# One inference layer on one core: the order of a few steps in the start-up, and the engine for one addition

## The chip, the core and the metric

The kernel runs on one core of a Trainium2 chip. The core has TensorE (PE in the profile), which multiplies matrices out of SBUF into PSUM, three engines that work on vectors, VectorE (DVE), ScalarE (ACT) and GpSimd (POOL), and SyncE (SP), whose queue issues most transfers. Each engine runs its own list of instructions in order; semaphores hold an instruction back until what it needs is there. The metric is the time of one execution in microseconds on the device, as the median of the runs.

## The reference

One layer of a decoder trunk, for a prompt of 1024 rows and 8 sample rows, 1024 columns wide (`D`). The parts that the change touches are the norm of x, the projection into `u, v, z_a, ...` and the product of the per-layer embedding p with `w_ple`:

```python
xn = _rmsnorm(h, pre_g)
proj = jnp.einsum('bld,de->ble', xn, w_in)
u, v, z_a, x_b, z_b, g_a, g_b = jnp.split(proj, SPLITS, axis=-1)
...
h = h + _rmsnorm(jnp.einsum('bld,de->ble', m, w_out), post_g)
e = jnp.einsum('blp,pd->bld', p, w_ple)
gate = jax.nn.sigmoid(jnp.einsum('bld,de->ble', _rmsnorm(h, ple_in_g), w_pg))
h = h + _rmsnorm(gate * e, ple_out_g)
```

Between them stand a gated mix along chunks of 128 rows, a pooling branch over trailing windows, and two projections that are merged by sigmoid gates. All is in float32.

## The kernel before, in words

**Tiling.** x comes as eight tiles of 128 rows (`x_89` to `x_92` are the last four, in the names that the built program gives) and one of the 8 sample rows (`xe_84`). Each row is scaled by the root of its mean square (`norm_root`, `norm_scale`, L853 to L859): ScalarE squares and sums, VectorE adds epsilon, GpSimd takes the root (`rstd`), VectorE scales the tile in place. The scaled tiles are turned by TensorE against an identity matrix, so that the contraction lies along the partitions. `x_half(j, kp)` (L872) does this for four tiles (`j` = 0: rows 0 to 511, 1: rows 512 to 1023) and two blocks of 128 columns (`kp` = 0 to 3, called first to fourth block here): eight transposes into PSUM. The result is called `pst`.

**Precision and products.** A float32 operand is split into two parts: a high one that ScalarE rounds (`xB11h`, `ph`, `wehi`), and the rest, the low one, that VectorE makes (`xB11l`, `pl`, `welo`). A product takes three matmuls, high by high, low by high and high by low. The large projections are done as seven products of sums of quarters instead of eight products of quarters. So the kernel needs both the parts of x's quarters and x's quarters as wholes, for the sums: the wholes lie in the buffer `big`. `x_out` (L900) writes a whole from PSUM on ScalarE (`big<-pst`), `x_whole` (L906) adds a high and a low part back together on GpSimd (`big<-xB11h,xB11l`), for x's first half of columns and rows. `xB22h` and `xB22l` are the parts of the second half of both.

**The sample's row.** `x_extra` (L911) turns the eight sample rows into one bank of PSUM (`pxe`), and VectorE multiplies them by the norm's gains into `big`, in four instructions. `x_tail` (L919) splits them into high and low parts.

**p and its product.** `p_turn(1, q)` turns p's second half, rows 512 to 1023, four transposes into one bank (`pp`); ScalarE and VectorE make `ph` and `pl` of it. `embed(t)` multiplies tile t's part by `w_ple` into a region of PSUM (`e`, 12 matmuls), and `embed_out(t)` copies it out, on ScalarE unless another engine is given. For tile 4 it is `nc.vector`.

**PSUM.** Two kinds of buffers are handed out in turn as they are asked for: three regions of two banks (`acc`, `e`, `pst` of the blocks 2 to 4), and two single banks (`pxe`, `pp`, `pst` of the first block). Who asks for a buffer waits for the last use of the one it gets.

**The weights of v.** VectorE makes sums of loaded weights (`vs<-vraw`) and low parts (`vw<-vraw,vw` or `vw<-vs,vw`), ScalarE the high parts. Products of x's parts with `vw` go to `acc`; `steps[n].evacuate()` copies them out (`v<-acc`). `steps[2]` and `steps[3]` are one product of each of the first two pairs of v's columns; in the built program the second pair's product lies in `acc_186` and its copy in `v_195`.

**What sets the order.** All operations go through a class `Planner`, whose call at L301 issues them, so that every instruction has line L301. What `begin()` (L1743) calls is fixed: each engine plays it in the order in which it was written. What comes after `plan.fixed = False` is put in order by the planner's own costs and due times. The place of the change is in the last third of `begin()`.

Of the kernel before, what the change touches and what calls it, by code (L numbers as in the profile page):

```python
# [13 lines left out]
ALU = mybir.AluOpType  # L14
# [7 lines left out]
HALF = 512  # L22
# [285 lines left out]
def hybrid_step(  # L308
# [7 lines left out]
    nc = tc.nc  # L316
# [24 lines left out]
    def bank(name):  # L341
        n_name[0] += 1
        return plan.tile(bankp.tile([P, 512], F32, tag="bank", name=f"{name}_{n_name[0]}"), "bank")

    def region(name):

        n_name[0] += 1
        return plan.tile(accp.tile([P, 2, 512], F32, tag="acc", name=f"{name}_{n_name[0]}"), "acc")
# [3 lines left out]
    def split(src, hi, lo):  # L352

        nc.scalar.activation(out=hi, in_=src, func=AF.Copy)
        nc.vector.tensor_tensor(out=lo, in0=src, in1=f32(hi), op=ALU.subtract)
# [4 lines left out]
    def add(out, a, b):  # L360
        nc.vector.tensor_tensor(out=out, in0=a, in1=b, op=ALU.add)
# [12 lines left out]
    nc = plan  # L374
# [43 lines left out]
    def quarter(kp, j):  # L418
        both = big[:, 2 * kp : 2 * kp + 2, :].rearrange("p a t -> p (a t)")
        return (both[:, 2 * HALF :] if j else both[:, : 2 * HALF]).rearrange("p (k t) -> p k t", k=2)  # L420
# [449 lines left out]
    col = lambda i, k: gvec[:, i * NB + k : i * NB + k + 1]  # L870

    def x_half(j, kp):  # L872

        if kp == 0:
            ps = [bank("pst") for _ in range(2)]
        else:
            ps = region("pst")
            ps = [ps[:, kk] for kk in range(2)]
        for kk in range(2):
            k = 2 * kp + kk  # L880
            for i in range(4):
                nc.tensor.transpose(ps[kk][:, i * P : (i + 1) * P], xts[4 * j + i][:, k * P : (k + 1) * P], ident)
        if j and kp < 2:
            turned[j, kp] = ps
            return
        hi, lo = x_parts(j, kp)
        for kk in range(2):
            nc.scalar.activation(out=hi[:, kk, :HALF], in_=ps[kk], func=AF.Copy, scale=col(0, 2 * kp + kk))
        for kk in range(2):
            nc.vector.scalar_tensor_tensor(out=lo[:, kk, :HALF], in0=ps[kk], scalar=col(0, 2 * kp + kk),  # L890
                                           in1=f32(hi[:, kk, :HALF]), op0=ALU.mult, op1=ALU.subtract)
        turned[j, kp] = ps

    turned = {}

    def x_parts(j, kp):
        what = f"B{kp // 2 + 1}{j + 1}"
        return xop.parts[what, kp % 2] if (what, kp % 2) in xop.parts else xop.new(what, kp % 2)

    def x_out(j, kp):  # L900

        for kk, ps in enumerate(turned.pop((j, kp))):
            o, gain = quarter(kp, j)[:, kk, :HALF], col(0, 2 * kp + kk)
            nc.scalar.activation(out=o, in_=ps, func=AF.Copy, scale=gain)

    def x_whole(j, kp):  # L906

        hi, lo = (f32(x[:, :, :HALF]) for x in xop.parts[f"B{kp // 2 + 1}{j + 1}", kp % 2])
        nc.gpsimd.tensor_tensor(out=quarter(kp, j)[:, :, :HALF], in0=hi, in1=lo, op=ALU.add)

    def x_extra():  # L911
        ps = bank("pxe").rearrange("p (k t) -> p k t", k=NB)
# [6 lines left out]
    def x_tail():  # L919
        for kp in range(2, NB // 2):  # L920
            split(quarter(kp, 1)[:, :, HALF:], *(x[:, :, HALF:] for x in x_parts(1, kp)))
# [410 lines left out]
    steps = [vsteps[i][j] for pairs in ((0, 1), (2, 3)) for j in range(2) for i in pairs]  # L1332
# [367 lines left out]
    def embed_terms(t, n, terms):  # L1700

        if t == 2:
            e_ps[t, n] = e_ps.get((t, n)) or bank("e")
        elif t not in e_ps:
            e_ps[t] = region("e")
        out = e_ps[t, n] if t == 2 else e_ps[t][:, n]
        todo = left.setdefault((t, n), 6)
        for k, (i, j) in terms:
            nc.tensor.matmul(out, pcut[t // 4][i][:, k, t % 4 * P : (t % 4 + 1) * P], we.at(n, k)[j],
                             start=todo == 6, stop=todo == 1)  # L1710
            todo -= 1
        left[t, n] = todo

    def embed(t):
        for n in range(2):
            embed_terms(t, n, [(0, HH), (0, HL), (0, LH), (1, HH), (1, HL), (1, LH)])

    def embed_out(t, by=None):
        e = slot("e", (P, 2, HALF))
        if t == 2:  # L1720
            for n in range(2):
                nc.scalar.activation(out=e[:, n], in_=e_ps.pop((t, n)), func=AF.Copy)
        elif by is None:
            nc.scalar.activation(out=e, in_=e_ps.pop(t), func=AF.Copy)
        else:
            by.tensor_copy(out=e, in_=e_ps.pop(t))
        r = t // 2 * 2 * P
        dma(kept["e"][r : r + 2 * P].rearrange("(p i) (n c) -> i p n c", i=2, n=2)[t % 2], e)
# [14 lines left out]
    def begin():  # L1743
        psl = slot("psamp", (P, PLE))
        p_load(0, 0)
        for i, v in enumerate((pre_g, pool_scale, ple_in_g)):
            dma(vecs[i * NB : (i + 1) * NB, :], v[0].rearrange("(k p) -> k p", p=P), nc.scalar)
        we.fetch(0)
        we.fetch(1)
        p_load(0, 1)  # L1750
        for t in range(4):
            x_load(t)
        dma(xe[:NS], x_sample)
        steps[0].loads()
        steps[1].loads()
        for t in range(4, NB):
            x_load(t)
        for q in range(2):
            p_load(1, q)
        dma(psl[:NS], p_sample)  # L1760
        praw.append(psl)
        fetched[0] = 6
        early_loads()

        def busy(n):
            ps = region("warm")[:, 0]
            for _ in range(n):
                nc.tensor.matmul(ps, junk[:, :P], junk, start=True, stop=True)

        p_new(0)  # L1770
        busy(5)
        we.high(0, 0)
        p_turn(0, 0, (0,), nc.vector)
        busy(1)
        p_turn(0, 0, (1,))
        we.high(0, 1)
        for k in range(2):
            we.low(0, k)
        for k in range(2):
            for i in (HH, LH):  # L1780
                for t in range(2):
                    embed_terms(t, 0, [(k, i)])
        for t in range(2):
            embed_terms(t, 0, [(0, HL), (1, HL)])
        for k in range(2):
            we.high(1, k)
        for k in range(2):
            we.low(1, k)
        vps = bank("vecs")
        nc.tensor.transpose(vps[:, : 3 * NB], vecs[: 3 * NB, :], ident[: 3 * NB, : 3 * NB])  # L1790
        nc.vector.tensor_copy(gvec, vps[:, : 3 * NB])
        embed_terms(0, 1, [(0, HH), (0, LH), (1, HH), (1, LH)])
        p_turn(0, 1)
        embed_terms(0, 1, [(0, HL), (1, HL)])
        embed_terms(1, 1, [(0, HH), (0, LH), (1, HH), (1, LH), (0, HL), (1, HL)])
        norm_root(0)
        norm_root(1)
        norm_scale(0)
        embed(2)
        norm_root(2)  # L1800
        embed_out(0, nc.vector)
        norm_root(3)
        norm_scale(1)
        norm_scale(2)
        embed_out(1)
        embed(3)
        norm_scale(3)
        embed_out(2)
        vweights[0].prepare("A11")
        embed_out(3, nc.vector)  # L1810
        for kp in range(3):
            x_half(0, kp)
        vweights[1].prepare("A11")
        x_half(0, 3)
        steps[0].run()
        vweights[0].prepare("A12")
        vweights[1].prepare("A12")
        norm_root(4)
        steps[0].evacuate()
        steps[1].run()  # L1820
        norm_root(S)
        norm_root(5)
        steps[1].evacuate()
        norm_scale(4)
        norm_root(6)
        norm_scale(S)
        norm_root(7)
        for t in range(5, NB):
            norm_scale(t)
        x_whole(0, 0)  # L1830
        x_whole(0, 1)
        steps[2].run()
        steps[2].evacuate()
        x_out(0, 3)
        x_out(0, 2)
        steps[3].run()
        for t in (8, 4, 5):
            steps[t].loads()
        steps[8].loads = None
        x_extra()  # L1840
        steps[3].evacuate()
        p_new(1)
        p_turn(1, 0)
        x_half(1, 2)
        p_turn(1, 1)
        x_half(1, 3)
        x_tail()
        embed(4)
        x_out(1, 2)
        x_half(1, 0)  # L1850
        x_out(1, 0)
        embed_out(4, nc.vector)
        x_out(1, 3)
        x_half(1, 1)
        x_out(1, 1)
        vweights[0].add_up()
        xop.combine("T3")
        embed(5)
        embed_out(5)
        prepared[0] = 4  # L1860
# [52 lines left out]
```

## Time and profile before

| | |
|---|---|
| three runs | 979.62, 979.65 and 981.12 us, median 979.65 |
| the profiled execution | 980.18 us |
| its span, first to last instruction | 978.4 us |
| mean clock granted to TensorE in it | 0.996 of full speed |
| instructions of PE, DVE, ACT, POOL | 6077, 1263, 899, 143 |

All times in the profile are microseconds from the start of the span. A row of a timeline gives start, duration, engine, line, operation, output and inputs, the size (partitions by elements) and the count of instructions that were put together; in square brackets stand the idle time before it and what ended that. Instructions of an engine overlap at their ends, so a duration is a little more than the distance from one start to the next. A granted clock of 0.50 is half speed.

### The profile page before, as it was taken

How to read it: one execution, taken by the hardware profiler on the slowest of the kernel's cores; microseconds unless marked ns; L12 is line 12 of the kernel's file. 1: busy time of each engine (PE TensorE's matmuls, PEld its weight loads, DVE VectorE, ACT ScalarE, POOL GpSimd, SP SyncE). 2: the span in 40 equal slices, each digit the busy share in tenths (PEclk: the TensorE clock that was granted, in tenths of full speed). 3: DMA queues.
4: the chain of work that ended last, by engine and by line, in shares of the span. 5: the costliest groups of instructions: out<-in, count | busy, mean ns of one | idle time of the engine just before them, and what ended most of it. 6: DMA issues, size and time to landing. Idle time of an engine off the chain costs nothing. (4 is left out here: it accounts for less than half of the span.)

```text
span 978.4 us, 16078 instructions
## 1 busy us (share of the span) xinstructions
PE 964.9 (99%) x6077; PEld 860.4 (88%) x6077; DVE 799.1 (82%) x1263; ACT 532.3 (54%) x899; POOL 73.2 (7%) x143
## 2 busy tenths in 40 slices
PE   9999999999999999999999999999999999999996
PEld 6789999999999999999999999999999986888775
DVE  6796658887789698979897987697799799769786
ACT  6775998865444433344543333552363273967662
POOL 1400000000000000001000100000000001312222
PEclk9999999999999999999999999999999999999999
DMA  9445572422483253656735167884583393799966
GB/s 334 160 151 129 135 171 87 167 94 78 141 298 130 95 187 118 242 196 221 258 131 173 37 228 249 273 312 151 176 302 107 126 349 97 169 280 363 292 183 194
DMA packets 119308, 185.56 MB, mean 190 GB/s; under 512 B 29183, under 2 KB 75735, under 8 KB 119222
## 3 DMA queue, kind: packets, MB, share of 16 engines
q1 hardware_dynamic: 117102, 177.11, 53.8%
q0 software_dynamic: 2080, 7.41, 4.3%
q8 instruction: 48, 0.79, 0.3%
q14 instruction: 30, 0.25, 0.1%
q10 hardware_dynamic: 48, 0.01, 0.0%
HBM read 125.85 MB, written 53.87 MB: 184 GB/s over the span
## 5 line engine op out<-in xcount | busy, mean ns | idle before, releaser
L301 DVE TENSOR_TENSOR u<-acc,u 128x520 f32<-128x520 f32 (+1 forms) x84 | 58.3, 695 | 23.8 <-PE acc L301 21.9
L301 POOL TENSOR_TENSOR rstd<-ms,mhalf 128x1 f32<-128x1 f32 (+1 forms) x36 | 29.7, 825 | 230.1 <-DVE ms L301 208.7
L301 POOL MEMSET u<- 128x8 f32 x32 | 3.3, 104 | 491.3 <-PE acc L301 232.2
L301 ACT ACTIVATE u<-acc 128x512 f32<-128x512 f32 x36 | 21.4, 594 | 23.7 <-PE acc L301 23.1
L301 ACT ACTIVATE paw<-pas 128x512 fp32r<-128x512 f32 x16 | 10.1, 628 | 30.7 <-DVE pas L301 25.5
L301 ACT ACTIVATE pbw<-pbs 128x512 fp32r<-128x512 f32 x16 | 10.0, 629 | 29.3 <-DVE pbs L301 26.1
L301 DVE TENSOR_TENSOR v<-acc,v 128x520 f32<-128x520 f32 (+1 forms) x20 | 13.9, 693 | 12.8 <-PE acc L301 12.6
L301 ACT ACT_TABLE_LOAD x17 | 21.8, 1283 | 4.3 <-PE acc L301 1.8
L301 DVE TENSOR_TENSOR big<-big 128x1024 f32<-128x1024 f32 (+4 forms) x20 | 23.7, 1217 | 0.0
L301 ACT ACTIVATE big<-v 128x1024 uint16<-128x1024 uint16 x16 | 18.6, 1170 | 7.2 <-DMA v<-vw 7.2
L301 PE MATMUL accm<-qh,wpoolw 128*128 128x260 f32 (+1 forms) x96 | 20.9, 320 | 0.0
L301 ACT ACTIVATE zbw<-zbs 128x512 fp32r<-128x512 f32 x16 | 10.0, 628 | 16.5 <-DVE zbs L301 10.2
L301 ACT ACTIVATE gbw<-gbs 128x512 fp32r<-128x512 f32 x16 | 10.0, 624 | 15.7 <-DVE gbs L301 13.7
L301 DVE TENSOR_TENSOR big<-mix,big 128x256 f32<-128x256 f32 x32 | 12.7, 419 | 6.9 <-ACT big L301 6.8
L301 ACT ACTIVATE big<-mix 128x256 f32<-128x256 f32 x32 | 11.7, 379 | 12.4 <-PE mix L301 12.0
L301 DVE TENSOR_TENSOR acc<-acc,u 128x512 f32<-128x512 f32 (+1 forms) x16 | 11.2, 699 | 8.8 <-PE acc L301 8.8
L301 ACT ACTIVATE uw<-us 128x512 fp32r<-128x512 f32 x16 | 10.0, 626 | 14.0 <-DVE us L301 6.8
L301 ACT ACTIVATE vw<-v 128x1024 uint16<-128x1024 uint16 x16 | 16.2, 1045 | 2.3 <-DVE v L301 2.3
L301 PEld LDWEIGHTS accm<-qh,wpoolw 128*128 128x128 f32 x96 | 15.6, 188 | 1.9
L301 ACT ACTIVATE u<-u 128x1032 f32<-128x1032 f32 (+1 forms) x8 | 6.8, 853 | 18.9 <-DVE u L301 18.8
L301 ACT ACTIVATE gb<-gb 128x1032 f32<-128x1032 f32 (+1 forms) x8 | 6.8, 854 | 18.5 <-DVE gb L301 18.5
L301 ACT ACTIVATE zaw<-zas 128x512 fp32r<-128x512 f32 x16 | 10.1, 629 | 12.4 <-PE acc L301 5.2
(666 smaller groups left out, 3599.7 us busy)
## 6 DMA issues: line engine op xcount, KB each, us to landing
ga<-ga SPq DMA_DIRECT2D x16, 516.0 KB
gb<-gb SPq DMA_DIRECT2D x16, 516.0 KB
vraw<-in_w_in_dram SPq DMA_DIRECT2D x22, 256.0 KB
ya<-za SPq DMA_DIRECT2D x8, 516.0 KB
yb<-zb SPq DMA_DIRECT2D x8, 516.0 KB
x<-in_x_prompt_dram SPq DMA_DIRECT2D x8, 512.0 KB
e<-e SPq DMA_DIRECT2D x8, 512.0 KB
garaw<-in_w_in_dram SPq DMA_DIRECT2D x8, 512.0 KB
```

The source lines that it names most:

```text
L301: getattr(getattr(self.nc, e), method)(*args, **kwargs)
```

## The change

- `x_half` is cut in two: `x_turn`, the transposes, and `x_cut`, the parts on ScalarE and VectorE. Elsewhere `x_half` still calls both in a row.
- `x_whole` adds on VectorE instead of GpSimd. Its first call comes after `x_extra` (before: after the scales of x's tiles), its second after `x_tail`.
- `steps[3].evacuate()` is called ahead of `x_extra` instead of behind it.
- The third block of x's second half is turned ahead of p's second half, and its fourth block between p's two groups; the parts are made where they were made before.
- The copy of tile 4's `e` goes to ScalarE, and is asked for one place earlier.

```diff
     def x_half(j, kp):
+        x_turn(j, kp)
+        x_cut(j, kp)
+
+    def x_turn(j, kp):
...
+        turned[j, kp] = ps
+
+    def x_cut(j, kp):
+
         if j and kp < 2:
-            turned[j, kp] = ps
             return
-        hi, lo = x_parts(j, kp)
+        ps, (hi, lo) = turned[j, kp], x_parts(j, kp)
...
-        turned[j, kp] = ps
...
-        nc.gpsimd.tensor_tensor(out=quarter(kp, j)[:, :, :HALF], in0=hi, in1=lo, op=ALU.add)
+        add(quarter(kp, j)[:, :, :HALF], hi, lo)
...
         for t in range(5, NB):
             norm_scale(t)
-        x_whole(0, 0)
-        x_whole(0, 1)
...
         steps[3].run()
+        steps[3].evacuate()
...
         x_extra()
-        steps[3].evacuate()
+        x_whole(0, 0)
+        x_turn(1, 2)
         p_new(1)
         p_turn(1, 0)
-        x_half(1, 2)
+        x_cut(1, 2)
+        x_turn(1, 3)
         p_turn(1, 1)
-        x_half(1, 3)
+        x_cut(1, 3)
         x_tail()
+        x_whole(0, 1)
         embed(4)
         x_out(1, 2)
         x_half(1, 0)
+        embed_out(4)
         x_out(1, 0)
-        embed_out(4, nc.vector)
```

What that does to the engines' lists is seen in the built programs. TensorE before, from the sample's transposes (`pxe_207`) on; `pp_210` and `pp_214` are p's two groups, `pst_211` x's third block:

```order
L301 MATMUL pxe_207<-ident,xe_84 128x8 x8
L301 MATMUL pp_210<-ident,p_124 128x128 x4
L301 MATMUL pst_211<-ident,x_89 128x128
L301 MATMUL pst_211<-ident,x_90 128x128
L301 MATMUL pst_211<-ident,x_91 128x128
L301 MATMUL pst_211<-ident,x_92 128x128
L301 MATMUL pst_211<-ident,x_89 128x128
```

TensorE now, from the same place; the third block is `pst_208`, p's first group `pp_211`, the fourth block `pst_214`:

```order
L301 MATMUL pxe_207<-ident,xe_84 128x8 x8
L301 MATMUL pst_208<-ident,x_89 128x128
L301 MATMUL pst_208<-ident,x_90 128x128
L301 MATMUL pst_208<-ident,x_91 128x128
L301 MATMUL pst_208<-ident,x_92 128x128
L301 MATMUL pst_208<-ident,x_89 128x128
L301 MATMUL pst_208<-ident,x_90 128x128
L301 MATMUL pst_208<-ident,x_91 128x128
L301 MATMUL pst_208<-ident,x_92 128x128
L301 MATMUL pp_211<-ident,p_124 128x128 x4
L301 MATMUL pst_214<-ident,x_89 128x128
```

The third block has moved ahead of p's first group, and the fourth ahead of its second. `pp_211` waits for the same multiplies of `pxe_207` on VectorE as `pp_210` did, since it has the same bank.

VectorE at that place, the difference of its list (`x_92` is x's last tile, `e_221` the copy of tile 4's `e`):

```order
 L301 TENSOR_SCALAR x_92<-x_92,rstd_203 128x1024
 L301 TENSOR_TENSOR big<-pxe_207,gvec 128x2x8 x4
-L301 TENSOR_TENSOR pl_209<-pp_210,ph_208 128x2x256
-L301 SCALAR_TENSOR_TENSOR xB22l_213<-pst_211,gvec,xB22h_212 128x512 x2
-L301 TENSOR_TENSOR pl_209<-pp_214,ph_208 128x2x256
-L301 SCALAR_TENSOR_TENSOR xB22l_217<-pst_215,gvec,xB22h_216 128x512 x2
+L301 TENSOR_TENSOR big<-xB11h_166,xB11l_167 128x1024
+L301 TENSOR_TENSOR pl_210<-pp_211,ph_209 128x2x256
+L301 SCALAR_TENSOR_TENSOR xB22l_213<-pst_208,gvec,xB22h_212 128x512 x2
+L301 TENSOR_TENSOR pl_210<-pp_215,ph_209 128x2x256
+L301 SCALAR_TENSOR_TENSOR xB22l_217<-pst_214,gvec,xB22h_216 128x512 x2
```

One addition is new there, behind the multiplies; the rest keeps its order under new numbers. Further down the second addition takes the place of the copy `e_221`, which stands on ScalarE now, behind its copies of the third block (`big<-pst_208`). GpSimd's two additions are gone from its list, between its last root and its first memset (of an end of `v`). ScalarE's copy `v_195<-acc_186` has not moved: it stands behind the copies `big<-pst_171` and ahead of `ph` in both programs, though it is now written ahead of the sample's row. SyncE's list is the same.

## The prediction

> **What bounds the kernel now.** I read the page first, then the waits of PE, then the timeline around PE's longest wait. The page gives the span and the busy time of each engine.
>
> ```profile
> span 978.4 us, 16078 instructions
> PE 964.9 (99%) x6077; PEld 860.4 (88%) x6077; DVE 799.1 (82%) x1263; ACT 532.3 (54%) x899; POOL 73.2 (7%) x143
> ```
>
> PE is busy for 99% of the span, so time can be won only where PE stops or runs slowly. The waits of PE over the whole run, with the total, the number and the longest of each:
>
> ```profile
> PE pp L301 <- issue: 2.3, 1, 2.3
> PE warm L301 <- DVE junk L301: 1.3, 1, 1.3
> PE e L301 <- ACT wehi L301: 1.0, 1, 1.0
> ```
>
> Only the first lies where the change is: PE stops once, for 2.3 us, ahead of p's second half (`pp`). The releaser is given as "issue", so the timeline must name it. PE's rows there:
>
> ```profile
> 33.32 0.66 PE L301 MATMUL pxe<-ident,xe 8*128 8x8 f32 x8
> 36.30 1.09 PE L301 MATMUL pp<-ident,p 128*128 128x128 f32 x4 [2.32 <-issue]
> 37.17 1.91 PE L301 MATMUL pst<-ident,x 128*128 128x128 f32 x8
> 38.88 0.85 PE L301 MATMUL pp<-ident,p 128*128 128x128 f32 x4
> 39.56 1.04 PE L301 MATMUL pst<-ident,x 128*128 128x128 f32 x8
> 40.35 0.48 PE L301 MATMUL e<-wehi,ph 128*128 128x512 f32 x1
> ```
>
> And what VectorE and GpSimd do at that time:
>
> ```profile
> 31.69 1.42 DVE L301 TENSOR_SCALAR x<-x,rstd 128x1024 f32<-128x1024 f32 x2
> 33.18 2.69 DVE L301 TENSOR_SCALAR x<-x,rstd 128x1024 f32<-128x1024 f32 x1
> 35.79 0.41 DVE L301 TENSOR_TENSOR big<-pxe,gvec 128x16 f32<-128x16 f32 x4
> 32.82 5.26 POOL L301 TENSOR_TENSOR big<-xB11h,xB11l 128x1024 f32<-128x1024 f32 x2
> ```
>
> The sample's transposes end at 33.98 (33.32 + 0.66). `pp` reuses their bank, so it waits until VectorE's four multiplies have read them, at 36.20 (35.79 + 0.41). These queue behind VectorE's last scale of x, which takes 2.69 us where two others take 1.42 together (0.71 to 0.75 each). All of it lies beside GpSimd's adds of x's halves. So the stall is GpSimd's add, passed on: add, slow scale, late multiplies, late bank.
>
> Then the clock. Columns: length, busy time and count of each engine, granted clock, DMA share, GB/s.
>
> ```profile
> 5.24:8.65 3.41, 2.38 (x10) 1.64 (x10) 2.43 (x6) 2.26 (x4) 0.00 (x0) 1.00 1.03 381
> 18.89:22.31 3.42, 3.42 (x31) 3.36 (x30) 3.31 (x6) 3.25 (x6) 0.00 (x0) 1.00 1.02 395
> 22.31:25.72 3.41, 3.41 (x15) 2.50 (x14) 3.41 (x7) 3.41 (x7) 0.00 (x0) 1.00 1.07 340
> 32.54:35.95 3.41, 1.44 (x12) 0.93 (x10) 3.34 (x4) 2.27 (x5) 3.41 (x3) 1.00 0.88 232
> 35.95:39.37 3.42, 3.08 (x15) 3.11 (x16) 0.93 (x4) 0.84 (x2) 2.71 (x18) 0.50 0.06 12
> 43.66:79.00 35.34, 35.34 (x207) 30.90 (x206) 35.16 (x47) 23.46 (x36) 0.00 (x0) 1.00 0.41 130
> ```
>
> From 35.95 to 39.37 PE gets half its clock; in the other rows it gets all of it. The stretch before, of the same 3.41 us, has PE busy for only 1.44; one with 2.38 busy (5.24 to 8.65) is not followed by half a clock. So the stall is paid twice: as idle time, and as 24 transposes at half speed.
>
> **The change, part by part.** *The stall.* The adds leave GpSimd, so the last scale should take 0.75 and end at 33.93 instead of 35.87. x's third block (8 transposes) now comes ahead of p's and needs no bank of the sample's; its fourth transpose is the first to need that scale. How long a transpose takes at full clock:
>
> ```profile
> 18.38 3.65 PE L301 MATMUL pst<-ident,x 128*128 128x128 f32 x32
> 21.79 0.48 PE L301 MATMUL acc<-xB11h,vw 128*128 128x512 f32 x1
> ```
>
> 32 of them fill 18.38 to 21.79, so 0.107 each. The fourth is due at 33.98 + 3 x 0.107 = 34.30, 0.37 after the scale. The multiplies then end at 34.45, and `pp` comes at 33.98 + 8 x 0.107 = 34.84, 0.39 after them. The stall goes whole: **2.32 us**.
>
> *The clock.* 24 transposes now take 36.30 to 40.35, 4.05 us; at full clock 24 x 0.107 = 2.56. That saves **1.49 us**. The lower bound comes from the 16 transposes in the next row, which take 1.89 with their changes of bank (0.118 each): 4.05 - 24 x 0.118 = 1.22.
>
> [...]
>
> *The sum.* 2.32 + 1.49 = 3.81, if nothing else is late: `e`'s first product then starts at 36.54 instead of 40.35.
>
> *What is next late.* Rows of PE, VectorE and ScalarE after the gap:
>
> ```profile
> 43.22 1.91 PE L301 MATMUL pst<-ident,x 128*128 128x128 f32 x16
> 45.11 0.50 PE L301 MATMUL e<-wehi,ph 128*128 128x512 f32 x1
> 42.35 1.40 DVE L301 SCALAR_TENSOR_TENSOR xB22l<-pst,gvec,xB22h 128x512 fp32r<-128x512 f32 x2
> 43.66 0.25 DVE L301 TENSOR_TENSOR xB22l<-big,xB22h 128x16 fp32r<-128x16 f32 x2
> 43.83 1.22 DVE L301 COPY e<-e 128x1024 f32<-128x1024 f32 x1
> 44.97 0.68 DVE L301 TENSOR_TENSOR vs<-vraw 128x512 f32<-128x512 f32 x1
> ```
>
> ```profile
> 37.48 0.60 ACT L301 ACTIVATE ph<-pp 128x512 fp32r<-128x512 f32 x1 [2.67 <-PE pp L301]
> 40.28 0.60 ACT L301 ACTIVATE ph<-pp 128x512 fp32r<-128x512 f32 x1
> 40.76 1.28 ACT L301 ACTIVATE xB22h<-pst,gvec 128x512 fp32r<-128x512 f32 x2
> 41.90 0.34 ACT L301 ACTIVATE xB22h<-big 128x16 fp32r<-128x16 f32 x2
> 42.11 1.29 ACT L301 ACTIVATE big<-pst,gvec 128x512 f32<-128x512 f32 x2
> 48.26 1.03 ACT L301 ACTIVATE e<-e 128x1024 f32<-128x1024 f32 x1 [0.82 <-PE e L301]
> ```
>
> ScalarE: `ph` followed `pp`'s end (37.39) by 0.09, so now it starts at 34.84 + 4 x 0.107 + 0.09 = 35.36. From start to start, by these rows, `ph` costs 0.48, a pair of highs 1.14, the two small ones 0.21, the two copies of a block 1.14. The string ph, highs, ph, highs, small ones, block copies is 0.48 + 1.14 + 0.48 + 1.14 + 0.21 + 1.14 = 4.59, so the copy of `e`, which the change moves here from VectorE, starts at 39.95 and ends at 40.98. PE needs that bank 45.11 - 40.35 = 4.76 after `e`'s start, at 41.30: 0.32 to spare. The last 8 transposes of the row at 43.22 need the block's region half a row earlier, at 36.54 + 2.87 + 0.95 = 40.36; its copies end at about 40.1, some 0.25 to spare. So this edit costs nothing, but a delay of 0.3 us on ScalarE would show.
>
> VectorE: the first add (taken at 1.22, by the row at 43.83, VectorE's work on the same 1024 columns) runs 34.4 to 35.65, ahead of `pl`, which cannot start before `ph` ends at 35.96: hidden. After it `pl` (0.68, like the 128x512 of the row at 44.97), lows 1.40, `pl`, lows, small ones 0.25 follow without a gap, each some 0.08 under the one before, to about 40.6. The second add takes the very place and 1.2 us of the copy of `e` that left. `vs` then starts at about 41.7 instead of 44.97: 3.25 earlier, not 3.81. The next rows show two weights of VectorE's and PE's first use of each:
>
> ```profile
> 66.24 0.68 DVE L301 TENSOR_TENSOR vw<-vraw,vw 128x512 fp32r<-128x512 f32 x1
> 70.96 0.62 PE L301 MATMUL acc<-xT4h,vw 128*128 128x512 f32 x2
> 75.22 0.69 DVE L301 TENSOR_TENSOR vw<-vs,vw 128x512 fp32r<-128x512 f32 x1
> 76.61 0.63 PE L301 MATMUL acc<-xT2h,vw 128*128 128x260 f32 x4
> ```
>
> That matters, since VectorE works 35.16 of the 35.34 us from 43.66 to 79.00, and PE uses what it makes. The closest use I found: `vw` ends at 75.91 (75.22 + 0.69) and PE reads it at 76.61, 0.70 later. The shortage of 3.81 - 3.25 = 0.56 leaves 0.14 of it. So VectorE just keeps up. Further on, the order differs only in two weights that VectorE makes one step later and one evacuation that ScalarE does one step earlier. I take these at nothing: one step is 0.7 to 1.2, and the first of those weights ends at 66.92, 4.0 ahead of its use at 70.96. PE stops nowhere, so the rest shifts as a whole.
>
> *The copy of the second pair,* written ahead of the sample's row, stands at the same place on ScalarE in both built orders, and the sample's row and p's first group share one bank as before. It costs nothing and gains nothing.
>
> *GpSimd's memsets* came after its adds and now come right after its last root, beside the scale that was slow:
>
> ```profile
> 38.06 0.56 POOL L301 MEMSET rc<- 128x1 f32 x15
> ```
>
> At worst they hold the scale for all of their 0.56 us, which is 0.2 more than its 0.37 to spare; at best not at all, as tiny writes. I take nothing, and keep 0.2 for the range. SP's transfers keep their order.
>
> **The rivals.** *The clock is not won.* Either the median run, unlike the profiled one, never lost it, since the 3.41-us stretches can fall otherwise in another run: then 3.81 - 1.49 = 2.32 are won. Or transposes don't count as work for the clock: then the stretch from 32.54 still holds only the 0.8 us of products up to 33.32, the next one stays at half, and at half clock 3.41 us lose 1.7: 2.1 are won. Off the two starting times that is 977.3 to 978.1. Against the second: 18.89 to 22.31 is nearly all transposes, and the stretch after it has clock 1.00. [...] Together 0.14.
>
> *VectorE or ScalarE is late in part.* A margin of 0.14 to 0.39 breaks for one or two of the four places above, and 0.2 to 2 of the gain go back as new stops: 977.5 to 979.5. 0.07.
>
> *The change doesn't do what it says.* The scale stays slow for another reason than the add. Then the fourth transpose waits until 35.87, a gap of 1.57, and 21 transposes at half clock follow to about 39.7: 0.65 won, 979.2. For it: the row names no cause. Against it: its two neighbours, without the add, took half of 1.42. 0.04.
>
> *Slower: VectorE becomes the bound.* Its string from `vs` to the `vw` at 75.22 doesn't start earlier (a late load of v's weights would do it). Then PE stops there, for 3.81 - 0.70 = 3.1 us, and, as at 33.98, a clock of one half follows, for 1.5 (as above) to 1.7 (half of 3.41): 3.8 - 3.1 - 1.6 = -0.9, 980.9. It decides from where the string is less than about 1 us earlier. Against it: the DMA share is down to 0.06 from 35.95 to 39.37, so those loads should be in. 0.03.
>
> **How the numbers follow.** The profiled execution took 980.18 us and the median of the runs is 979.65, 0.53 less. 980.18 - 3.81 = 976.4, and 979.65 - 3.81 = 975.8; I give 976.1, with 0.72. Own range: 975.3 (the median's figure and another 0.53) to 976.9 (the profiled figure with 0.27 less for the clock and 0.2 for the memsets). To leave out no more than 2 in 10 it must take in the clock rival: 975.3 to 978.1. 0.2%, about what a measurement of this kernel can tell from no change, is 1.96 us, so faster means below 977.69: the forecast, half of the clock rival and a little of the third, 0.82. Same: the other half, most of the partial cases and the 0.04: 0.14. Slower: 0.04.
>
> **What would show it.** Right: the scale ahead of the sample's multiplies takes 0.75; PE has no wait at `pp`; the granted clock is 1.00 from 32 to 43; `e` starts 3.8 earlier against the sample's transposes. The steps are wrong one by one if the scale still takes over 2 us; if the clock falls with no gap; or if the waits of PE show a new entry, at `e` or `pst` for ScalarE or at `acc` for `vw`. A time above 978.1 would make the prediction wrong.

## The result, and the profile after

The changed kernel takes 975.82 us (median of six runs, 975.26 to 976.12) where the kernel before takes 979.63: 3.81 us less, a ratio of 0.9958 with the 95% interval 0.9945 to 0.9971. In two later sets of runs, each beside the kernel before, it was 2.77 and 3.81 us faster. The profiled execution took 976.12 us, with a span of 974.4.

The waits of TensorE in it. The stop of 2.3 us at `pp` is gone, and no other of its kind has come into the list:

```profile
PE warm L301 <- DVE junk L301: 1.3, 1, 1.3
PE pp L301 <- DMA p<-in_p_prompt_dram: 0.2, 1, 0.2
```

(The `pp` of 0.2 is p's first half, in the first 10 us. The wait for `wehi` in the kernel before, 1.0 there, lies in the first 10 us too; it hangs on a load (ScalarE stands idle 0.99 for it), and over the traces it was anything from too short for the list to 1.2.)

TensorE at the place of the change:

```profile
33.19 0.66 PE L301 MATMUL pxe<-ident,xe 8*128 8x8 f32 x8
33.78 1.09 PE L301 MATMUL pst<-ident,x 128*128 128x128 f32 x8
34.71 0.60 PE L301 MATMUL pp<-ident,p 128*128 128x128 f32 x4
35.15 1.04 PE L301 MATMUL pst<-ident,x 128*128 128x128 f32 x8
36.02 0.60 PE L301 MATMUL pp<-ident,p 128*128 128x128 f32 x4
36.38 0.48 PE L301 MATMUL e<-wehi,ph 128*128 128x512 f32 x1
...
39.25 2.06 PE L301 MATMUL pst<-ident,x 128*128 128x128 f32 x16
41.13 0.50 PE L301 MATMUL e<-wehi,ph 128*128 128x512 f32 x1
```

The sample's transposes end at 33.85 (33.19 + 0.66) and `e` starts at 36.38. These two times make the measure that I use for every kernel below: **2.53 us** now, 6.37 before (33.98 to 40.35). The other 13.2 us up to the first `acc` that follows, and the 925 us behind that, are as they were.

The clock, over the time in which it had fallen before (length, busy time and count of each engine, granted clock, DMA share, GB/s):

```profile
33.00:36.00 3.00, 3.00 (x30) 2.79 (x29) 2.41 (x6) 2.26 (x6) 0.46 (x18) 1.00 0.90 239
36.00:39.40 3.40, 3.40 (x20) 2.78 (x19) 2.90 (x5) 3.40 (x9) 0.00 (x0) 1.00 0.10 25
39.40:42.80 3.40, 3.40 (x24) 2.91 (x22) 3.37 (x7) 3.40 (x7) 0.00 (x0) 1.00 0.25 104
```

VectorE, with the scale that had taken 2.69 as the last of the first row's three, and GpSimd:

```profile
31.55 2.45 DVE L301 TENSOR_SCALAR x<-x,rstd 128x1024 f32<-128x1024 f32 x3
33.92 0.40 DVE L301 TENSOR_TENSOR big<-pxe,gvec 128x16 f32<-128x16 f32 x4
34.25 1.21 DVE L301 TENSOR_TENSOR big<-xB11h,xB11l 128x1024 f32<-128x1024 f32 x1
36.04 0.69 DVE L301 TENSOR_TENSOR pl<-pp,ph 128x512 fp32r<-128x512 f32 x1 [0.58 <-ACT ph L301]
...
41.74 0.68 DVE L301 TENSOR_TENSOR vs<-vraw 128x512 f32<-128x512 f32 x1
```

```profile
32.66 0.35 POOL L301 MEMSET v<- 128x8 f32 x1
32.70 0.72 POOL L301 MEMSET rc<- 128x1 f32 x15
```

Three scales from 31.55 to 34.00; the multiplies follow at once, and the addition stands in the gap ahead of `pl`.

### The profile page after: what moved, and what is told of

It reads as the page before. It is cut to its first block, busy times and chain, and to the rows that moved or that the text cites. A ratio compares the mean times of both kernels' runs of the same rounds, so it can differ in the third digit from the quotient of the medians.

```text
span 974.4 us, 16073 instructions
## 1 busy us (share of the span) xinstructions
PE 964.2 (99%) x6077; PEld 859.2 (88%) x6077; DVE 798.1 (82%) x1264; ACT 533.9 (55%) x900; POOL 67.9 (7%) x141
```

## The experiments

**The theory:** GpSimd's first addition holds VectorE's last scale, this the multiplies, these the bank that p's first group needs; TensorE stops for 2.3 us and then pays again with half a clock. **The rivals:** the order on TensorE (p ahead of the block) is what cost the time, wherever the addition runs; the half clock has another cause than the stop, or no part in the gain. The table gives the time from the sample's transposes to `e` in each trace, and the medians with those of the kernel before in the same set.

| kernel | to `e` | median | before | ratio, 95% |
|---|---|---|---|---|
| before, again | 6.43 | 980.24 | 980.68 | 0.9989 to 1.0008 |
| changed | 2.53 | 975.82 | 979.63 | 0.9945 to 0.9971 |
| changed, second | 2.53 | 976.96 | 979.73 | 0.9953 to 0.9978 |
| changed, third | 2.53 | 976.87 | 980.68 | 0.9951 to 0.9979 |
| p first | 3.16 | 977.47 | 979.74 | 0.9963 to 0.9980 |
| p first, again | 3.15 | 976.49 | 979.73 | 0.9954 to 0.9979 |
| additions on GpSimd | 5.88 | 978.28 | 979.74 | 0.9976 to 0.9992 |
| copy on VectorE | 2.53 | 977.93 | 979.74 | 0.9965 to 0.9987 |
| sample's transposes x4 | 6.40 | 979.32 | 979.74 | 0.9985 to 1.0002 |
| stop filled, transposes | 4.80 | 978.77 | 979.73 | 0.9978 to 0.9996 |
| stop filled, products | 4.91 | 979.29 | 979.73 | 0.9982 to 1.0000 |
| additions in place | 4.11 | 977.91 | 979.51 | 0.9969 to 0.9989 |
| scale on ScalarE | 2.68 | 976.59 | 979.51 | 0.9962 to 0.9985 |

In the row with the sample's transposes four times over, the time is taken from the end of the first eight.

**1. The order undone** (`e1_p_first`, from the changed kernel):

```diff
         x_whole(0, 0)
-        x_turn(1, 2)
         p_new(1)
         p_turn(1, 0)
-        x_cut(1, 2)
-        x_turn(1, 3)
+        x_half(1, 2)
         p_turn(1, 1)
-        x_cut(1, 3)
+        x_half(1, 3)
```

> The changed kernel with the old order on TensorE: p's first group ahead of x's third block, its second ahead of the fourth; the additions stay on VectorE behind the sample's multiplies, and the copy of tile 4's e stays on ScalarE. Theory (the stall was GpSimd's addition, passed on through the last scale of x): the scale takes 0.75, the multiplies end at about 34.4, and TensorE stops at pp for about 0.45 us only, with the clock at 1.00: 0.2 to 0.5 above the changed kernel, 976.0 to 976.4. Rival (the order on TensorE is what took the stall away): a stop of about 2.3 and a stretch of half clock as before, 979 to 980.

977.47, above the range, in two groups (976 and 978). Once more, beside the changed kernel:

> The changed kernel once more, for the comparison on this chip, since the kernel with p's order undone fell into two groups of times (976 and 978) where 976.0 to 976.4 was expected. Theory: 975.3 to 976.3, with no stop between the sample's transposes and e, and the clock at 1.00. Rival (the spread belongs to the day's runs, not to that kernel): a spread of 2 us here too.

> The changed kernel with p's order undone, again. Theory: from the end of the sample's transposes to e 3.2 us where the changed kernel has 2.5, clock 1.00, so 0.6 above the changed kernel's median in the same call; the rest of the spread lies in the first 33 us and in waits for the weights of the gate at 180 to 195 us. Rival (a stop of 0.6 costs half a clock in a part of the executions): two groups again, 1.5 to 1.7 apart, with the upper one showing a granted clock of 0.50 for 3.4 us.

The changed kernel spread over 2 us here too (975.63 to 977.67, the median above its range), and p first came out at 976.49, with overlapping intervals. The second trace of p first shows why it costs so little:

```profile
33.28 0.66 PE L301 MATMUL pxe<-ident,xe 8*128 8x8 f32 x8
34.52 0.63 PE L301 MATMUL pp<-ident,p 128*128 128x128 f32 x4 [0.59 <-PE pxe L301]
```

The stop is 0.59: the scale ends 0.16 behind the sample's transposes, and VectorE's multiplies take 0.40. The granted clock stays at 1.00 behind it in both traces (to 42.8 and 41.0 us). So moving the addition is worth 3.2 of the 3.8 us, and the new order 0.6, of which 0.4 is left at the first `acc`: from `e` to there p first takes 13.0 in both traces and the changed kernel 13.2 in all three. The rival, that a stop of 0.59 takes half a clock in some executions, finds no support in the runs either: all 16 of p first have a mean clock of 0.997 or 0.998, in the upper group as in the lower (the end of 4 says what such a mean tells). What parts the two groups stays open.

**2. The additions back on GpSimd** (`e2_add_on_gpsimd`):

```diff
-        add(quarter(kp, j)[:, :, :HALF], hi, lo)
+        nc.gpsimd.tensor_tensor(out=quarter(kp, j)[:, :, :HALF], in0=hi, in1=lo, op=ALU.add)
```

> The changed kernel with only the two additions back on GpSimd. Theory: the last scale of x takes about 2.7 again, the fourth transpose of x's third block waits for it, a stop of about 1.5 us, and a stretch of half clock follows: about 0.7 won of 3.8, 978.8 to 979.3. Rival (the new order alone takes the stall away, since the block needs no bank of the sample's): 975.8 to 976.5.

978.28. TensorE and VectorE:

```profile
33.17 0.55 PE L301 MATMUL pst<-ident,x 128*128 128x128 f32 x3
35.19 0.91 PE L301 MATMUL pst<-ident,x 128*128 128x128 f32 x5 [1.47 <-DVE x L301]
```

```profile
30.95 4.18 DVE L301 TENSOR_SCALAR x<-x,rstd 128x1024 f32<-128x1024 f32 x3
```

Three transposes, then a stop of 1.47 for the tile that the slow scale holds, and half a clock:

```profile
35.67:39.08 3.41, 3.41 (x18) 3.41 (x17) 0.94 (x2) 1.75 (x3) 2.24 (x18) 0.50 0.07 18
```

The rival falls. Against the kernel before, the stretch to `e` is 0.5 shorter, and the way to the first `acc` 0.7, as expected. The median is 1.46 lower, twice that and below the range. A part of it may be the clock: 8 of these 12 executions have a mean clock of 0.997 or more, so they seem not to have paid the half clock that the trace shows (see the end of 4).

**3. The copy of `e` back on VectorE** (`e3_copy_on_vector`):

```diff
-        embed_out(4)
+        embed_out(4, nc.vector)
```

> The changed kernel with only the copy of tile 4's e back on VectorE. In the built program tile 5's product then gets the region of x's fourth block, and tile 6's that of the copied e. Theory (three places are tied, and 1.2 us more on VectorE breaks one): ScalarE ends the copies of the fourth block at about 42.4, so TensorE stops at e for about 1.2, VectorE's weights come 1.2 later as well and stop nothing more: 976.8 to 977.2, clock at 1.00. Rival (the margins of VectorE and ScalarE are wider than they seem): 975.6 to 976.1.

977.93, above the range by 0.7; the trace has the stop where it was expected:

```profile
39.51 2.08 PE L301 MATMUL pst<-ident,x 128*128 128x128 f32 x16
42.81 0.50 PE L301 MATMUL e<-wehi,ph 128*128 128x512 f32 x1 [1.22 <-ACT big L301]
```

So the move of this copy is no decoration: without it the next product gets the region of x's fourth block, and waits 1.22 us for ScalarE's copies of that block. The granted clock is 1.00 up to this stop (39.4 to 42.8), and the mean of 0.998 over the span speaks against half a clock behind it (see the end of 4).

**4. The clock by itself.** Three kernels leave the stop's cause alone and give TensorE something to do in it. The sample's own transposes, over again (`e4_fill_stall`):

```diff
-        for k in range(NB):
+        for k in 4 * list(range(NB)):
             nc.tensor.transpose(ps[:, k, :NS], xe[:NS, k * P : (k + 1) * P], ident[:NS, :NS])
```

> The kernel before, with the eight transposes of the sample's rows done four times over into the same places (32 for 8), so that TensorE has transposes to do through its stop of 2.3 us; the stop's cause is untouched. Theory (idle time in one stretch of 3.41 us takes half the clock in the next): the granted clock stays 1.00 from 36 to 39, the 24 transposes take 2.6 instead of 4.05, p's first group starts 0.1 to 0.2 later: 978.2 to 978.5 where before has 979.6. Rival (transposes do not count as work for the clock, or the clock falls for another reason): 0.50 again, 979.6 to 979.9.

979.32, no difference that can be measured from the kernel before. The two stretches of 3.41 us, the second with half a clock:

```profile
31.92:35.33 3.41, 2.88 (x36) 2.38 (x34) 3.34 (x5) 2.24 (x5) 3.41 (x3) 1.00 0.90 239
35.33:38.74 3.41, 3.08 (x15) 3.12 (x16) 0.92 (x4) 0.85 (x2) 2.68 (x18) 0.50 0.10 25
```

TensorE was busy for 2.88 of 3.41 and still lost the clock, where 2.38 of other work had kept it (5.24 to 8.65 in the kernel before). So in this trace the transposes of 8 by 8 did not count as that other work did. Larger ones, then (`e7_fill_transposes`; `e8_fill_products` has 8 times `matmul(spare[:, 0], hi[:, 0, :P], hi[:, 0, :HALF])` there, with `hi` the first high part of x; lines that are not shown make `x_half(1, 2)` turn into the buffer that `early` names):

```diff
         x_extra()
+        spare = region("pst")
+        early[1, 2] = [spare[:, kk] for kk in range(2)]
+        for _ in range(18):
+            nc.tensor.transpose(spare[:, 0, :P], xts[4][:, 4 * P : 5 * P], ident)
         steps[3].evacuate()
```

> The kernel before, with 18 transposes of 128 x 128 (x's fifth tile, over and over, into the place that x's third block overwrites) put into TensorE's stop behind the sample's row. They take 1.9 of its 2.3 us and stop nothing else. Theory (transposes of this size are work for the clock, the sample's of 8 rows are not): no stretch of half clock, the 24 transposes take 2.6 instead of 4.05, 1.3 to 1.5 won: 978.1 to 978.5. Rival (no transpose counts): half a clock from 35 to 36 on for 3.4 us, and the time of before, 979.5 to 980.

> The kernel before, with 8 products of 128 x 512 (a high part of x by itself, into the place that x's third block overwrites) put into TensorE's stop behind the sample's row, 1.9 of its 2.3 us. Theory (idle time takes the clock): clock 1.00 from 33 to 43 and 1.3 to 1.5 won, 978.1 to 978.5, the same as with transposes. Rival (the clock's half stretch has another cause there, such as the transposes that follow): 0.50 again and 979.5 to 980.

978.77 and 979.29. Both lie above their ranges, and the second's interval reaches 1.0000. The trace of the first, with the clock at 1.00 from 33.0 to 42.8, as in that of the second:

```profile
33.87 2.18 PE L301 MATMUL pst<-ident,x 128*128 128x128 f32 x18
36.17 0.63 PE L301 MATMUL pp<-ident,p 128*128 128x128 f32 x4
36.63 1.04 PE L301 MATMUL pst<-ident,x 128*128 128x128 f32 x8
37.51 0.60 PE L301 MATMUL pp<-ident,p 128*128 128x128 f32 x4
37.94 1.04 PE L301 MATMUL pst<-ident,x 128*128 128x128 f32 x8
38.74 0.48 PE L301 MATMUL e<-wehi,ph 128*128 128x512 f32 x1
```

From `pp` to `e` 2.57 instead of 4.05, with p's group as late as ever: the half clock costs 1.48 in the stretch, and as much by the other kernel (36.66 to 39.23). Work in the stop takes the penalty away, and transposes of 128 by 128 do as well as products. The medians moved by less, 0.96 and 0.44. Both traces give 0.2 back at a wait for the copy of `e`, the second 0.3 more at a weight of the gate; the rest is not explained.

*Did every execution pay?* The mean granted clock of each execution is on record, and it speaks against that. The four traces with a stretch of 0.50 have a mean of 0.995 or 0.996 over the span, the ten without have 0.997 or 0.998. (My estimate of why that sorts them: the trace of the kernel before has 0.50 for its last 3.8 us too, that of the changed kernel for its last 4.2; 3.8 alone make a mean of 0.998, and with 3.41 more it comes out at 0.9963. The line isn't quite sharp: the one of 7 below has no such stop in its trace.)

| kernel | executions with a mean of 0.996 or less |
|---|---|
| before, in the sets of the experiments | 69 of 98 |
| sample's transposes x4 | 5 of 11 |
| additions on GpSimd | 4 of 12 |
| scale on ScalarE | 1 of 7 |
| changed, p first, copy on VectorE, additions in place, stop filled | 0 of 72 |

So some 3 in 10 executions of the kernel before seem to have kept their clock through the stop. There is no trace of one, and what parts them from the others is not shown. In the four sets the medians of those executions are 0.0, 0.4, 0.6 and 1.8 us below those of the others. So the totals do not confirm the 1.48 of the stretch as a price that each execution pays. And with 6 of 11 executions on the side that kept it, where the kernel before has 3 in 10, the small transposes can't be said to count for nothing.

**5. Only the engine changed, on the kernel before** (`e9_add_in_place`, the same line as in 2, the other way round, with the calls where they were).

> The kernel before with only the engine of x_whole changed: both additions on VectorE where they were written, ahead of the sample's multiplies; order on TensorE and copy of e as before. In the built program p's first group gets the bank of the second pair then, and its second group that of the sample. Theory (the time of a step is when VectorE gets to the multiplies): the scale takes 0.75, the multiplies end at 36.6 behind 2.4 us of additions, TensorE stops for 0.9 at p's first group (for the second pair's copy) and 0.5 at its second, keeps the clock, and e starts 2.4 earlier than before: about 2.4 won. Rival (moving the additions to VectorE is worth the whole gain wherever they stand): 3.4 to 3.8 won. Other rival (the additions ahead of the multiplies hold p as much as the slow scale did): 0 to 0.5 won.

977.91: 1.6 won by the median, 2.27 in the stretch.

```profile
34.18 0.66 PE L301 MATMUL pp<-ident,p 128*128 128x128 f32 x4 [0.87 <-ACT v L301]
34.67 1.04 PE L301 MATMUL pst<-ident,x 128*128 128x128 f32 x8
36.16 0.63 PE L301 MATMUL pp<-ident,p 128*128 128x128 f32 x4 [0.45 <-PE pst L301]
```

Two stops, 0.87 for the second pair's copy and 0.45 for the multiplies behind 2.3 us of additions. P first, with the additions behind the multiplies, is 0.95 shorter in the stretch. It also has another bank for p's first group, the sample's, so the place and the bank are not told apart.

**6. GpSimd keeps the additions, ScalarE takes the scale** (`e10_scale_on_scalar`, from the changed kernel, with the line of 2 as well):

```diff
-        for t in range(5, NB):
+        for t in range(5, NB - 1):
             norm_scale(t)
...
         x_out(0, 3)
+        nc.scalar.activation(out=xts[7], in_=xts[7], func=AF.Copy, scale=roots.pop(7))
         x_out(0, 2)
```

> The changed kernel with both additions back on GpSimd and, in their stead, the scale of x's last tile on ScalarE, between its copies of two blocks. So GpSimd's additions run beside the same work of VectorE less that scale. Theory (of what VectorE has to do there only the scale of a tile in SBUF is held up by GpSimd; its work on PSUM is not): the multiplies take 0.4 as before, from the sample's transposes to e 2.5 to 2.7, clock 1.00, and ScalarE's string is 0.3 later, so at most 0.3 of stops at pst or e: 0 to 0.4 above the changed kernel. Rival (GpSimd's additions slow all of VectorE's work): multiplies and pl take twice as long and TensorE stops for 0.5 to 2 us at pp or e.

976.59, the changed kernel's time within the spread. VectorE and GpSimd:

```profile
33.97 0.42 DVE L301 TENSOR_TENSOR big<-pxe,gvec 128x16 f32<-128x16 f32 x4 [0.90 <-PE pxe L301]
36.45 0.69 DVE L301 TENSOR_TENSOR pl<-pp,ph 128x512 fp32r<-128x512 f32 x1 [2.06 <-ACT ph L301]
```

```profile
32.78 4.85 POOL L301 TENSOR_TENSOR big<-xB11h,xB11l 128x1024 f32<-128x1024 f32 x2
```

Beside GpSimd's additions the multiplies take 0.42 and `pl` 0.69; in the changed kernel, without them, it is 0.40 and 0.69. So the addition as such does no harm here; only the pair of it and the scale does. It is another way to the same gain, not a better one.

**7. Before and after, once more.** The totals in 1 to 6 had moved by up to 1 us less than the stretch, in 2 by 1 us more.

> The kernel before once more, for a second trace: in the other runs the totals moved by 0.5 to 1 less than the stretch between the sample's transposes and e did. Theory (the gain is that stretch, 3.8, and the rest is spread from the start-up's loads and from weights that land late): 6.3 to 6.4 from the sample's transposes to e, with a stop of 2.3 and 3.4 us of half clock again; 979.3 to 980.0. Rival (the stretches of the clock fall otherwise in some executions, and the kernel before then keeps its clock): about 4.9 there and no 0.50.

> The changed kernel a third time, beside a fresh trace of the kernel before. Theory: 2.5 from the sample's transposes to e, no half clock, 3 to 3.8 below the kernel before, with what is missing to 3.8 seen in the start-up or behind 125 us. Rival (the three places that are tied within 0.1 break in some executions): waits of PE at e, pst or acc between 36 and 80 us.

976.87 for the changed kernel beside 980.68: 3.81. The kernel before again, 980.24 and so 0.2 above its range, shows its stop and its half clock:

```profile
35.63 1.09 PE L301 MATMUL pp<-ident,p 128*128 128x128 f32 x4 [2.32 <-issue]
```

```profile
35.45:38.86 3.41, 3.23 (x16) 3.26 (x17) 0.77 (x3) 0.99 (x2) 2.54 (x18) 0.51 0.14 34
```

The same trace has these waits at the weights of the gate, `gaw`, at about 149 us, which the three of the changed kernel don't have:

```profile
PE acc L301 <- DVE gaw L301: 0.5, 1, 0.5
PE acc L301 <- ACT gaw L301: 0.2, 1, 0.2
```

Such waits come and go with no regard to the change (1.1 in one trace of p first, 0.5 in the other), and the sample's transposes end anywhere from 33.24 to 35.38. What moves the medians of one kernel by 1 us may lie there, and for the kernel before in the clock as well; in the traces the stretch to `e` repeats within 0.06.

## Why the prediction was right

**The stop.** Predicted 2.32 won, all of it; measured so. The chain from the addition to the bank holds: taking the addition off GpSimd (1) or the scale off VectorE (6) ends it alike. The kernel of 2, which is the changed one with the addition put back and that of 6 with the scale put back, has a stop again. The scale came out at 0.96 instead of 0.75:

```profile
33.04 0.96 DVE L301 TENSOR_SCALAR x<-x,rstd 128x1024 f32<-128x1024 f32 x1
```

GpSimd's memsets run beside it to 33.4; they were bounded at 0.56 and taken at nothing. I put the 0.21 down to them, though no run was made without them. The fourth transpose had 0.16 to spare instead of 0.37. The 34.45 for the end of the multiplies doesn't follow from the rows given (33.98 + 0.41 = 34.39); they ended at 34.32, and `pp` came 0.39 behind them, as forecast.

**The clock.** Predicted 1.49; the 24 transposes take 2.53 instead of 4.05, so 1.52, and experiment 4 finds 1.48 by itself, in two kernels. That is the price in the traces. Four traces (before twice, the additions on GpSimd, the sample's transposes four times) have stops of 0.85 to 2.32 us and a granted clock of 0.50 or 0.51 over 3.41 us that begin between 0.35 ahead of the stop's end and 0.48 behind it.

**The rival on the clock.** Its first form, an execution that never lost the clock, is no empty one: by the mean clock some 3 in 10 executions of the kernel before are of that kind. In each of the four sets the others were more than half, and every trace with a stop of 1.4 us or more there (2.32 twice, 1.47) shows the half clock; for the first set the means of the kernel before are not on record. The forecast took the loss as certain and gave this form and the next 0.14 together. That the gain wasn't smaller for it is partly luck. Its second form fell for transposes of 128 by 128: with 18 of them in the stop, 2.18 us, the clock stayed at 1.00. After 32 of 8 by 8, 2.14 us, it was 0.50, in one trace.

**What is next late.** The places were the right ones, the margins were taken too wide. ScalarE's copy of `e`:

```profile
40.01 1.08 ACT L301 ACTIVATE e<-e 128x1024 f32<-128x1024 f32 x1
```

It ends at 41.09 and TensorE takes the region at 41.13: 0.04, where 0.32 were forecast. The copy starts 0.06 later than worked out and takes 0.05 more, and TensorE comes 0.17 earlier; the sample's transposes already end 0.13 earlier. The term that was too small is `pp`: four steps of 0.107, 0.43, were allowed for it, but a group of four takes 0.60 to its last end, and `ph` waits for that end. VectorE's weight and its use:

```profile
71.99 0.68 DVE L301 TENSOR_TENSOR vw<-vs,vw 128x512 fp32r<-128x512 f32 x1
72.43 0.40 PE L301 MATMUL acc<-xT2l,vw 128*128 128x260 f32 x2
72.73 0.75 PE L301 MATMUL acc<-xT2h,vw 128*128 128x260 f32 x4
73.32 0.40 PE L301 MATMUL acc<-xT2l,vw 128*128 128x260 f32 x2
```

It ends at 72.67, and TensorE starts on it 0.06 later. That is no margin: TensorE waited for it. From the row ahead to the row behind it takes 0.89 here, and 0.72 in the kernel before:

```profile
76.36 0.40 PE L301 MATMUL acc<-xT2l,vw 128*128 128x260 f32 x2
77.08 0.41 PE L301 MATMUL acc<-xT2l,vw 128*128 128x260 f32 x2
```

So the 0.14 that were to be left had become a wait of 0.17 (0.17 and 0.26 in the other two traces of the changed kernel), too short for the list of waits. `vs` itself started at 41.74, where 41.7 was forecast. Experiment 3 shows what it costs when a place is missed outright: 1.22. The rival of a VectorE that is late in part had more of a case than its 0.07: it came true in the small, just under the 0.2 at which its price began.

**No effect.** The second pair's copy ahead of the sample's row: with that one line undone in the changed kernel, the built lists of all engines are the same, row for row.

**The sum.** 3.81 predicted, 3.81 measured in the first set. Over three sets it was 2.8 to 3.8, so the match to the hundredth is luck. The stretch's 3.84 repeats better, but it is read from two traces of the kernel before that both paid the half clock.

## What to carry to other kernels

When a saturated engine stops, follow the chain back past the engine that it waits for: here a scale of VectorE took 2.69 us beside an addition of GpSimd with which it shares no data, and 0.96 with the addition moved. Count the clock after a stop as part of its price; in the traces 1.5 us of 3.8 came from that. But one trace is one execution: look at the mean clock of the others before you count on it. And before work is moved to an engine that the next step waits for, list the margins behind it from the trace: here one of 0.70 became a wait of 0.17, and another is down to 0.04.

## What was unexpected in the hardware

A scale of VectorE took longer beside an addition of GpSimd, and a root of GpSimd took longer beside scales of VectorE. GpSimd in the kernel before, a root and the first addition:

```profile
31.90 1.24 POOL L301 TENSOR_TENSOR rstd<-ms,mhalf 128x1 f32<-128x1 f32 x1
32.82 2.49 POOL L301 TENSOR_TENSOR big<-xB11h,xB11l 128x1024 f32<-128x1024 f32 x1
```

The addition ends at 35.31 and VectorE's scale, begun at 33.18, at 35.87, 0.56 behind it: 2.69 in all, where the two scales ahead of it took 0.71 to 0.75 each. The root of 128 values takes 1.24 here, beside two of VectorE's scales, and 0.55 where none runs, in the changed kernel:

```profile
27.47 0.55 POOL L301 TENSOR_TENSOR rstd<-ms,mhalf 128x1 f32<-128x1 f32 x1 [9.99 <-DVE ms L301]
```

Not all work of VectorE was held: beside GpSimd's additions in 6 the multiplies and `pl`, each with an input in PSUM, took 0.42 and 0.69.
